# Loading the first row blocks of the output projection during the last head, and another order of its blocks

## The chip, the core and the metric

The program runs on one core of one Trainium2 chip. The metric is the device time of one execution in microseconds (us), the median of repeated runs. TensorE (PE) multiplies; its weight loads are a row of their own (PEld). VectorE (DVE), ScalarE (ACT) and GpSimd (POOL) do elementwise work, and SyncE (SP) issues most of the transfers (DMA). Each engine takes its instructions in the order of its own queue, so an instruction that waits holds up all that stand behind it on that engine.

## The reference, cut to what matters

One layer of a hybrid backbone on 512 latent tokens and 256 context tokens of width 1024, in float32. Two groups of four heads (a gated linear recurrence, "hg", and a gated delta rule, "dn") scan the tokens in both directions. Their normalised outputs are laid side by side and go through one output projection, a residual, and a mixture of 16 experts.

```
def hybrid_mixer(pc, px, lb, hg_norm_w, conv_w, a_log, dt_bias, dn_norm_w):
    ...
    hg_c, hg_x = hgrn2_branch(cols_c[:5], cols_x[:5], lb, hg_norm_w)
    dn_c, dn_x = deltanet_branch(cols_c[5:], cols_x[5:], conv_w, a_log, dt_bias, dn_norm_w)
    return jnp.concatenate([hg_c, dn_c], axis=-1), jnp.concatenate([hg_x, dn_x], axis=-1)
...
        xs = xs + g1x * (ox @ w_out[l])
        xs = xs + g2x * hierarchical_moe(modulate(rms_norm(xs, norm2_w[l]), sh2x, sc2x), *moe_args)
...
    return rms_norm(xs, final_norm_w)
```

`ox` is 512 x 1024 and `w_out` 1024 x 1024. A row block of `w_out` is 128 of its rows; blocks 0 to 3 belong to the four hg heads and blocks 4 to 7 to the four dn heads.

## The kernel before, in words

**Precision by parts.** A float32 product is made of three passes on TensorE: each operand is split into a rounded high part (a CAST on ACT) and the rest (a subtraction on DVE), and high x high, high x low and low x high are summed in PSUM. Whatever is multiplied so first needs one ACT and one DVE instruction per piece.

**Up to the projection.** The loop over heads (from L1071) runs the two scans of each head, with projections, gates (`gates`, names `z01...` and `sz`) and the rest of the modulation (`mod_rest`, tiles `wm`, L1001 loads and L1003 products) as filling. The scans' tiles live in the pool `dn`: `E` and `EB` (decay), `seg`, `kc`, `kt`, `t3`. `head_norm` (squares `nsq` on ACT L1038, a power on POOL L1045, the scaling on DVE L1047) writes the outputs in place into `ohg` and `odn`; for heads 2 and 3 this is done in the last round. After the heads the pools of the scan are closed (L1098), and `late`, `rt` and `fin` take their place.

**The output projection.** `KO` (L1109) is the order in which the eight row blocks are used, in four pairs: 0 1, 4 5, 2 3, 6 7. `channel_major` (L1111) transposes one head's output for a block on TensorE (`mt`, L1115), casts it to `mhi` (L1116) and subtracts to `mlo` (L1117). Its PSUM tile comes from the two buffers of `psG`, so a third transpose waits for the first one's `mlo`. `load_wo(nh, k2)` (L1124) loads one pair of row blocks of one half of the columns, 512 KB, into `wor` (two buffers, L1127), scales it by the gate `g1b` on DVE if it is the second half (L1130), and splits it into `woh` (L1132) and `wol` (L1134). The first half is multiplied pair by pair for four token tiles at once (L1286, PSUM `wo`, 96 products); the transposes of the last four blocks are placed behind its second pair. The second half goes token tile by token tile (L1345, 96 products), with the first half's transposes (`ptt`, L1250) and router logits (`plg`, L1258) put in between by hand. Then come the residual (L1230, L1235, L1236), the token rows `tt` written to DRAM (L1274 to L1276), the routing and the expert loop (L1404 and L1409 split weights, L1533 and L1571 multiply).

**What sets the order.** The Tile framework's scheduler orders each engine's queue from its own estimate of durations; `hi(...)` raises priority, `issue_after` and `add_manual_dep` set an order by hand. A tile put where a closed tile lay waits for the last use of that one. SP's queue carries the loads of `w_out`, the gate row `g1b` (L1141), the latent tokens `xs1` (L1143), small router rows (L1146 to L1153, `row2` among them, which TensorE transposes as `pr`, L1155), `w2b` (L1177) and the expert weights (L1204).

Of the kernel before, what the change touches and what calls it, by code (L numbers as in the profile page):

```python
# [9 lines left out]
F32 = mybir.dt.float32  # L10
F32R = mybir.dt.float32r
# [5 lines left out]
P = 128  # L17
# [203 lines left out]
def tile_kernel(ctx, tc, x, c, ctxt, c_ctx, w_mod, b_mod, norm1_w, norm2_w, w_in, w_out, hg_lb, hg_norm_w,  # L221
# [849 lines left out]
    for h in range(H):  # L1071
        with hi(HPS):
            dn_scan(h, *proj[h][:2], *prep[h][:3], prep[h][4])
        if h + 1 < H:
            with hi(HPD):
                prep[h + 1] = dn_prep(h + 1, *proj[h + 1], *dec[h + 1])
                dn_inv(h + 1, prep[h + 1][3])
        if h + 2 < H:
            dec[h + 2] = dn_decay(h + 2)
        with hi(HPG):  # L1080
            hg_head(h, vps[h // 2], *hpr[h])
        for f in FILL[h]:
            if f == "v":
                vps[1] = hg_values(1)
            elif f == "p":
                proj[h + 2] = dn_proj(h + 2)
            elif f == "q":
                hpr[h + 1] = hg_proj(h + 1)
            elif f in "01":
                sz[int(f)] = gates(int(f), h // 2)  # L1090
            elif f in "ab":
                mod_rest(1 + "ab".index(f))
            elif f in "no":
                for g in {"n": (h,), "o": (h - 1, h)}[f]:
# [11 lines left out]
    fin = mid.enter_context(tc.tile_pool(name="fin", bufs=1))  # L1106
    mhi = fin.tile([P, KB, SEQ], F32R, name="mhi")
    mlo = fin.tile([P, KB, SEQ], F32R, name="mlo")
    KO = (0, 1, 4, 5, 2, 3, 6, 7)  # L1109

    def channel_major(kb):  # L1111
        pt = psG(f"mt{kb}")
        src = (ohg, odn)[kb // 4]
        for t in range(NLT):
            nc.tensor.transpose(pt[:, t * P:(t + 1) * P], src[:, t, kb % 4, :], ident)  # L1115
        nc.scalar.copy(mhi[:, kb, :], pt)  # L1116
        nc.vector.tensor_sub(mlo[:, kb, :], pt, mhi[:, kb, :].bitcast(F32))  # L1117

    for kb in KO[:4]:
        channel_major(kb)  # L1120
    wos = [{}, {}]
    xs1 = late.tile([P, NLT, D], F32, name="xs1")

    def load_wo(nh, k2):  # L1124
# [7 lines left out]
        nc.scalar.copy(hi_, raw)  # L1132
        lo_ = fin.tile([P, 2, 512], F32R, tag="wol", name=f"wol{nh}_{k2}", bufs=NWO)
        nc.vector.tensor_sub(lo_, raw, hi_.bitcast(F32))  # L1134
        wos[nh][k2] = (hi_, lo_)
        return ld

    for k2 in KO[::2]:
        load_wo(0, k2 // 2)
    g1b = rt.tile([P, D], F32, name="g1b")  # L1140
    nc.sync.dma_start(g1b, mod_d[0].partition_broadcast(P))  # L1141
# [138 lines left out]
    for i, k2 in enumerate(KO[::2]):  # L1280
        hi_, lo_ = wos[0][k2 // 2]
        for t in range(NLT):
            ts_ = slice(t * P, (t + 1) * P)
            for k in range(2):
                for n, (m, w) in enumerate(((mhi, hi_), (mhi, lo_), (mlo, hi_))):
                    mm = nc.tensor.matmul(acc[t], m[:, k2 + k, ts_], w[:, k, :], start=(i == 0 and k == 0 and n == 0),  # L1286
                                          stop=(i == 3 and k == 1 and n == 2))
        if i == 1:
            with tc.issue_after(mm.ins):
                for kb in KO[4:]:  # L1290
                    channel_major(kb)
# [44 lines left out]
    for t in range(NLT):  # L1336
# [339 lines left out]
```

## Time and profile before

| what | value |
|---|---|
| median of 3 runs | 961.73 us (960.93 to 962.4) |
| the profiled execution | 960.25 us |
| its span, first to last instruction | 958.5 us |
| mean granted TensorE clock in it | 0.973 |
| PE busy, share of the span | 883.3 us, 92% |
| PEld | 722.3 us, 75% |
| DVE | 726.5 us, 76% |
| ACT | 501.6 us, 52% |
| POOL | 207.4 us, 22% |

Times are counted in the profiled execution from the span's start. The last head ends near 547 us, the two halves of the output projection run to 617 us, routing to about 632 us, and the experts to about 920 us. A granted clock of 1.0 is TensorE's 2.4 GHz and one of 0.5 is 1.2 GHz; a mean between them over a stretch is a mixture of the two.

### The profile page before, as it was taken

The page shows a single profiled execution, that of the slowest core. Times are in us where ns is not written, and L with a number is a line of the kernel's source. Part 1 is how long each engine was busy: PE and PEld are TensorE (multiplying, and loading weights), DVE is VectorE, ACT ScalarE, POOL GpSimd, SP SyncE. Part 2 cuts the span into 40 slices and gives each one's busy share as a digit, 9 for nine tenths or more (in the row PEclk, how much of TensorE's full clock was granted, in tenths as well). Part 3 has the DMA queues.
Part 4 walks back from the last instruction along what each step waited for, and adds up shares of the span by engine and source line. Part 5 has one row for each costly group of instructions (what it writes and reads, how often), then busy time and mean ns, then how long its engine had stood idle before and what let it go on. Part 6 is the DMA issues. An engine that isn't in the chain of part 4 may idle for free. (4 is left out here: it accounts for less than half of the span.)

```text
span 958.5 us, 20502 instructions
## 1 busy us (share of the span) xinstructions
PE 883.3 (92%) x8221; PEld 722.3 (75%) x8221; DVE 726.5 (76%) x1377; ACT 501.6 (52%) x966; POOL 207.4 (22%) x224
## 2 busy tenths in 40 slices
PE   3999998989879999799998989999999999999995
PEld 1688877878768887687895868867888887777772
DVE  2698489757899579964484566677989988888987
ACT  4445542454246344432432343127888888788862
POOL 2232631251135213412111110001111111010011
PEclk9999997999989999999999989999999999999997
DMA  9920350201102102038218278469999999999735
GB/s 313 315 67 23 111 198 24 69 22 41 30 23 52 38 25 56 12 116 251 79 51 278 70 249 327 158 248 377 382 364 365 372 368 361 374 370 363 294 129 146
DMA packets 116444, 180.03 MB, mean 188 GB/s; under 512 B 9975, under 2 KB 49459, under 8 KB 116216
## 3 DMA queue, kind: packets, MB, share of 16 engines
q1 hardware_dynamic: 109256, 163.49, 50.3%
q0 software_dynamic: 6480, 14.71, 4.6%
q8 instruction: 66, 1.08, 0.5%
q10 hardware_dynamic: 608, 0.47, 0.2%
q14 instruction: 34, 0.28, 0.1%
HBM read 170.31 MB, written 16.27 MB: 195 GB/s over the span
## 5 line engine op out<-in xcount | busy, mean ns | idle before, releaser
L1409 DVE TENSOR_TENSOR lo<-w,hi 128x1024 fp32r<-128x1024 f32 x184 | 216.8, 1222 | 27.1 <-ACT hi L1404 25.3
L1404 ACT CAST hi<-w 128x1024 fp32r<-128x1024 f32 x184 | 186.1, 1050 | 22.0 <-PE pu L1533 9.7
L1571 PE MATMUL py<-lo,ah 128*128 128x512 f32 x128 | 51.8, 404 | 0.7
L1571 PE MATMUL py<-hi,ah 128*128 128x512 f32 x128 | 50.8, 398 | 0.0
L1571 PE MATMUL py<-hi,al 128*128 128x512 f32 x128 | 49.4, 396 | 0.3 <-DVE al L1563 0.3
L1533 PE MATMUL pg<-lo,xh 128*128 128x512 f32 x120 | 48.7, 406 | 0.0
L1533 PE MATMUL pu<-lo,xh 128*128 128x512 f32 x120 | 48.3, 403 | 0.2 <-DVE lo L1409 0.2
L1533 PE MATMUL pg<-hi,xh 128*128 128x512 f32 x120 | 47.7, 397 | 0.0
L1533 PE MATMUL pu<-hi,xh 128*128 128x512 f32 x120 | 47.6, 396 | 0.0
L1533 PE MATMUL pg<-hi,xl 128*128 128x512 f32 x120 | 47.5, 396 | 0.0
L1533 PE MATMUL pu<-hi,xl 128*128 128x512 f32 x120 | 47.5, 396 | 0.0
L1389 POOL DMA_INDIRECT y_d<-y,cl x15 | 17.5, 1168 | 133.2 <-ACT y L1575 119.9
L815 POOL TENSOR_TENSOR am<-atr,cst 128x128 f32<-128x128 f32 x32 | 17.7, 557 | 123.4 <-PE po L818 108.5
L1382 POOL DMA_INDIRECT xg<-t_d,cl x15 | 18.4, 1230 | 115.9 <-PE xt L1521 106.1
L938 DVE TENSOR_TENSOR KS<-KS,F 128x384 f32<-128x384 f32 x56 | 32.3, 615 | 3.3 <-ACT km L901 2.8
L811 DVE TENSOR_SCALAR vs<-px,bs 128x128 f32<-128x128 f32 x48 | 16.6, 345 | 19.5 <-PE px L809 19.3
L1571 PEld LDWEIGHTS py<-lo,ah 128*128 128x128 f32 x128 | 24.1, 188 | 8.6 <-DVE lo L1409 3.3
L1003 PE MATMUL psm<-wm,cl 128*32 128x128 f32 x512 | 25.4, 284 | 4.8 <-DMA wm<-in_w_mod_dram 4.4
L562 DVE SCALAR_TENSOR_TENSOR qc<-lpad,cw,qc 128x512 f32<-128x512 f32 x32 | 29.4, 919 | 0.4
L1571 PEld LDWEIGHTS py<-hi,ah 128*128 128x128 f32 x128 | 24.1, 188 | 6.3 <-ACT ah L1562 0.6
L1571 PEld LDWEIGHTS py<-hi,al 128*128 128x128 f32 x128 | 24.2, 189 | 6.2 <-DVE al L1563 0.8
L1533 PEld LDWEIGHTS pu<-lo,xh 128*128 128x128 f32 x120 | 22.6, 188 | 7.9 <-DVE lo L1409 2.8
(1065 smaller groups left out, 2723.8 us busy)
## 6 DMA issues: line engine op xcount, KB each, us to landing
w<-in_w_gate_dram SPq DMA_DIRECT2D x32, 1024.0 KB, 15.1
w<-in_w_up_dram SPq DMA_DIRECT2D x32, 1024.0 KB, 14.9
w<-in_w_down_dram SPq DMA_DIRECT2D x32, 1024.0 KB, 16.5
wm<-in_w_mod_dram SPq DMA_DIRECT2D x64, 256.0 KB, 4.3
wm<-in_w_mod_dram SPq DMA_DIRECT2D x16, 512.0 KB, 8.3
y_d<-zt POOLq DMA_DIRECT2D x8, 512.0 KB, 7.7
wor<-in_w_out_dram SPq DMA_DIRECT2D x8, 512.0 KB, 5.1
xt<-in_x_dram SPq DMA_DIRECT2D x4, 512.0 KB, 9.9
```

The source lines that it names most:

```text
L562: nc.vector.scalar_tensor_tensor(al, s, w, al, op0=ALU.mult, op1=ALU.add)
L811: nc.vector.tensor_scalar(vs, px[:, 0:P], bs[:, d, i:i + 1], None, op0=ALU.mult)
L815: nc.gpsimd.tensor_mul(am, atr[:, t, :], K(("le", "ge")[d]))
L938: nc.vector.tensor_mul(kh, kh, tt(d, 1 - d))
L1003: nc.tensor.matmul(ps[32 * c_:32 * c_ + 32, P * j:P * j + P], cl[:, kb, :], raw[:, P * c_:P * c_ + P], start=(kb == 0), stop=(kb == KB - 1))
L1382: return nc.gpsimd.indirect_dma_start(out=dst, out_offset=None, in_=t_d[:, :], in_offset=bass.IndirectOffsetOnAxis(ap=idx, axis=0), bounds ...
L1389: i_ = nc.gpsimd.indirect_dma_start(out=y_d[:, :], out_offset=bass.IndirectOffsetOnAxis(ap=idx, axis=0), in_=src, in_offset=None, bounds_c ...
L1404: nc.scalar.copy(hi, raw)
L1409: s.append(lo_on.tensor_sub(s[1], raw, s[0].bitcast(F32)))
L1533: a_pu[0] = nc.tensor.matmul(ps, m[:, kb, :], ww[:, k, :], start=(kb == 0 and n == 0), stop=(kb == KB - 1 and n == 2))
L1571: mm = nc.tensor.matmul(ps, m[:, k, :], ww[:, k % 2, :], start=(k == 0 and n == 0), stop=(k == 3 and n == 2))
```

## The change

Two row blocks of the first column half, blocks 0 and 1, are no longer loaded by `load_wo`. Each is loaded alone (256 KB) into the scan's own buffers (`E` and `seg`) and split there (`EB` and `t3` for the high parts, `kc` and `kt` for the rest), in code that stands in front of the closing of the scan's pools. `load_wo` makes the other three pairs, in the order 4 5, 6 7, 2 3. The order of the blocks in both halves is 0 1 4 5 6 7 2 3. Six blocks (0, 1, 4, 5, 6 and 2) are transposed in front of the first half, and one each (7, then 3) behind its first and second pair. The split of the pair 4 5 is ordered by hand behind that of block 1. The weights are now indexed as lists of two blocks.

```
+    first_wo = [[], []]
+    for k in range(2):
+        raw = dn.tile([P, 512], F32, tag=("E", "seg")[k], name=f"wor_{k}")
+        nc.sync.dma_start(raw, w_out[k * P:(k + 1) * P, 0:512])
+        hi_ = dn.tile([P, 512], F32R, tag=("EB", "t3")[k], name=f"woh_{k}")
+        lo_ = dn.tile([P, 512], F32R, tag=("kc", "kt")[k], name=f"wol_{k}", bufs=2)
+        nc.scalar.copy(hi_, raw)
+        nc.vector.tensor_sub(lo_, raw, hi_.bitcast(F32))
+        first_wo[0].append(hi_)
+        first_wo[1].append(lo_)
     mix.close()
...
-    KO = (0, 1, 4, 5, 2, 3, 6, 7)
+    KO = (0, 1, 4, 5, 6, 7, 2, 3)
...
-    for kb in KO[:4]:
-        channel_major(kb)
-    wos = [{}, {}]
+    parts_of = [channel_major(kb) for kb in KO[:5] + KO[6:7]]
+    wos = [{0: first_wo}, {}]
...
+        if nh == 0 and k2 == KO[2] // 2:
+            for a_, b_ in zip((h_, l_), parts_of[1]):
+                tc.add_manual_dep(a_.ins, b_.ins.name, behind, reason="behind what is ready")
...
-    for k2 in KO[::2]:
+    for k2 in KO[2::2]:
         load_wo(0, k2 // 2)
...
-        if i == 1:
+        if i < 2:
             with tc.issue_after(mm.ins):
-                for kb in KO[4:]:
-                    channel_major(kb)
+                channel_major(KO[5 + 2 * i])
```

Lines behind the insertion have higher numbers in the changed kernel: L1116 is L1127 there, L1117 is L1128, L1130 is L1141, L1132 is L1143, L1134 is L1145, L1143 is L1157 and L1152 is L1166. Numbers at the end of a name tell tiles apart; `wor_0`, `wor_1`, `wor_2` and `wor_3` are the pairs 0 1, 2 3, 4 5 and 6 7.

On ACT, at the end of the last head, the queue before had the first pair's cast ahead of the first transposed block:

```order
L969 COPY kst_4_1_7139<-hpk_4_1_7137 128x128
L1132 CAST woh_0_7389<-wor_0_7387 128x1024
L1116 CAST mhi<-mt_7358 128x512
L1132 CAST woh_2_7395<-wor_2_7393 128x1024
L1116 CAST mhi<-mt_7365 128x512
L1038 ACTIVATE nsq_7314,nss_7315<-odn 128x128 x4
```

and with the change:

```order
L969 COPY kst_4_1_7139<-hpk_4_1_7137 128x128
L1127 CAST mhi<-mt_7370 128x512
L1127 CAST mhi<-mt_7377 128x512
L1143 CAST woh_2_7415<-wor_2_7413 128x1024
L1143 CAST woh_3_7421<-wor_3_7419 128x1024
L1038 ACTIVATE nsq_7314,nss_7315<-odn 128x128
L1127 CAST mhi<-mt_7384 128x512
```

Both transposed blocks now stand ahead of every weight cast there.

On DVE, in the middle of the first half, where the second half's first pair (`wor_0` with `g1b`) is scaled, before:

```order
L1047 SCALAR_TENSOR_TENSOR ohg<-ohg,nss_7329,sz_7151 128x128 x4
L1130 TENSOR_TENSOR wor_0_7447<-wor_0_7447,g1b 128x1024
L1157 COPY col_7428<-pr_7426 128x24
L1130 TENSOR_TENSOR wor_2_7454<-wor_2_7454,g1b 128x1024
L1159 COPY A_162<-col_7428 128x8
L1160 SCALAR_TENSOR_TENSOR A_162<-col_7428 128x8
L1117 TENSOR_TENSOR mlo<-mt_7557,mhi 128x512
L1134 TENSOR_TENSOR wol_0_7452<-wor_0_7447,woh_0_7450 128x1024
```

and with the change:

```order
L1047 SCALAR_TENSOR_TENSOR ohg<-ohg,nss_7329,sz_7151 128x128 x4
L1145 TENSOR_TENSOR wol_1_7429<-wor_1_7425,woh_1_7427 128x1024
L1141 TENSOR_TENSOR wor_0_7467<-wor_0_7467,g1b 128x1024
L1128 TENSOR_TENSOR mlo<-mt_7398,mhi 128x512
L1145 TENSOR_TENSOR wol_0_7472<-wor_0_7467,woh_0_7470 128x1024
L1128 TENSOR_TENSOR mlo<-mt_7405,mhi 128x512
L1128 TENSOR_TENSOR mlo<-mt_7553,mhi 128x512
L1128 TENSOR_TENSOR mlo<-mt_7584,mhi 128x512
L1141 TENSOR_TENSOR wor_2_7474<-wor_2_7474,g1b 128x1024
L1171 COPY col_7448<-pr_7446 128x24
```

One scaling instead of two stands ahead of the low parts of the late blocks, and the router's column (`col`) comes behind all of them.

On SP, the loads behind the gate row `g1b`, before:

```order
L1150 DMA rb<-in_b_expert_dram 128x16
L1152 DMA row_7423<-mod_d 16x128
L1153 DMA row_7423<-in_norm_w_dram 8x128
L1127 DMA wor_0_7447<-in_w_out_dram 128x2x512
L1127 DMA wor_2_7454<-in_w_out_dram 128x2x512
L1175 DMA sh_7475<-mod_d 128x1024
L1143 DMA xs_7386<-in_x_dram 128x1024 x4
```

and with the change:

```order
L1138 DMA wor_0_7467<-in_w_out_dram 128x2x512
L1155 DMA g1b<-mod_d 128x1024
L1160 DMA wrt<-in_w_group_dram 128x8x4
L1161 DMA wrt<-in_w_expert_dram 128x8x16
L1163 DMA rb<-in_b_group_dram 128x4
L1164 DMA rb<-in_b_expert_dram 128x16
L1157 DMA xs_7412<-in_x_dram 128x1024 x4
L1166 DMA row_7443<-mod_d 16x128
L1167 DMA row_7443<-in_norm_w_dram 8x128
L1138 DMA wor_2_7474<-in_w_out_dram 128x2x512
L1189 DMA sh_7495<-mod_d 128x1024
```

The second half's first pair moved ahead of `g1b`, and the four loads of the latent tokens moved ahead of the small `row` loads.

Further moves: on SP the two new loads stand in the first `mod_rest`, one behind its 6th load `wm` and one behind its 20th; `w2b` moves behind all five expert weights and behind `g2b` and `fw`. On TensorE `pr` stands behind 68 of the first half's 96 products, and the router's constant (`pcb`, L1167) moves from the first half into the second half's first tile. On DVE the token rows of the first two tiles, and the row `a2` (L1178) that they need, move behind the second half's second tile.

## Rows read from the trace of the kernel before

**Rows 1.** Stretches of the span (from : to and length in us), busy us and number of instructions of PE, PEld, DVE, ACT and POOL, then the granted clock, the DMA share and GB/s: the end of the last head and the first half of the output projection.

```profile
545.00:550.00 5.00, 3.04 (x24) 2.45 (x22) 2.63 (x10) 1.37 (x2) 0.68 (x1) 1.00 0.68 210
...
550.00:555.00 5.00, 4.79 (x16) 3.75 (x17) 4.15 (x8) 4.69 (x17) 1.04 (x1) 0.67 0.44 122
...
568.00:572.00 4.00, 1.16 (x7) 1.06 (x8) 4.00 (x7) 2.84 (x4) 2.00 (x1) 1.00 1.01 394
...
572.00:576.00 4.00, 4.00 (x14) 3.17 (x13) 2.40 (x4) 0.09 (x1) 0.00 (x0) 0.57 1.02 405
```

**Rows 2.** PE in order of time (start, us, what, how many; in brackets the idle time before it and what ended it): from the transposes of block 1 to the first products of the first half.

```profile
547.48 0.60 PE L1115 MATMUL mt<-cst,ohg 128*128 128x128 f32 x4
...
550.21 0.96 PE L1286 MATMUL wo<-woh,mhi 128*128 128x512 f32 x3 [2.13 <-ACT mhi L1116]
...
553.94 0.63 PE L1286 MATMUL wo<-woh,mhi 128*128 128x512 f32 x1
...
554.37 0.63 PE L1286 MATMUL wo<-wol,mhi 128*128 128x512 f32 x1
...
555.20 0.39 PE L1286 MATMUL wo<-woh,mhi 128*128 128x512 f32 x1
...
555.42 0.39 PE L1286 MATMUL wo<-wol,mhi 128*128 128x512 f32 x1
```

**Rows 3.** ACT in order of time in the same place, and the last two squares of the last head.

```profile
548.63 1.04 ACT L1132 CAST woh<-wor 128x1024 fp32r<-128x1024 f32 x1 [3.79 <-DMA wor<-in_w_out_dram]
...
549.58 0.58 ACT L1116 CAST mhi<-mt 128x512 fp32r<-128x512 f32 x1
...
555.65 0.31 ACT L1038 ACTIVATE nsq<-ohg 128x128 f32<-128x128 f32 x1
...
556.08 0.31 ACT L1038 ACTIVATE nsq<-ohg 128x128 f32<-128x128 f32 x1
...
556.30 0.18 ACT L1038 ACTIVATION_READ_ACCUMULATOR nsq<-ohg 128x1 f32 x1
```

**Rows 4.** SP's transfers in order of issue (start, time of the issues, line, number), and the last line of the answer on the tile `row`: from issue to landing.

```profile
544.00 7.32 SPq L1127 DMA_DIRECT2D wor<-in_w_out_dram  x3
...
556.51 0.34 SPq L1141 DMA_DIRECT2D g1b<-mod_d  x1
...
561.09 0.43 SPq L1152 DMA_DIRECT2D row<-mod_d  x1
...
563.50 2.40 SPq L1143 DMA_DIRECT2D xs<-in_x_dram  x4
...
571.85 2.35 SPq L1127 DMA_DIRECT2D wor<-in_w_out_dram  x2
...
577.57 0.90 SPq L1177 DMA_DIRECT2D w2b<-in_norm_w_dram  x1
...
DMA to landing us min/median/max: 2.4/2.4/2.4
```

**Rows 5.** PE in order of time: the second stop in the first half, what follows it, the second half's first product, and its first transposes.

```profile
566.83 0.39 PE L1286 MATMUL wo<-wol,mhi 128*128 128x512 f32 x1
...
570.84 0.63 PE L1115 MATMUL mt<-cst,odn 128*128 128x128 f32 x4 [3.62 <-DVE mlo L1117]
...
572.24 0.62 PE L1286 MATMUL wo<-woh,mhi 128*128 128x512 f32 x1
...
575.64 1.86 PE L1167 MATMUL pcb<-wrt,shb 128*128 128x20 f32 x16
...
584.20 0.39 PE L1345 MATMUL wo<-woh,mhi 128*128 128x512 f32 x1
...
587.41 0.66 PE L1250 MATMUL ptt<-cst,xs 128*128 128x128 f32 x4 [1.24 <-DVE xs L1236]
```

**Rows 6.** DVE in order of time: the scaling of the last hg head, the scaling of the second half's first pair, and the low part behind it.

```profile
560.31 1.13 DVE L1047 SCALAR_TENSOR_TENSOR ohg<-ohg,nss,sz 128x128 f32<-128x128 f32 x4
...
566.61 1.23 DVE L1130 TENSOR_TENSOR wor<-wor,g1b 128x1024 f32<-128x1024 f32 x1 [5.17 <-DMA wor<-in_w_out_dram]
...
570.02 0.68 DVE L1117 TENSOR_TENSOR mlo<-mt,mhi 128x512 fp32r<-128x512 f32 x1
```

**Rows 7.** DVE in order of time in the second half: the row `a2` (a pass over 128x1024), the residual of the first tile, and the last instructions ahead of the last residual.

```profile
593.19 1.22 DVE L1178 SCALAR_TENSOR_TENSOR a<-a,w2b 128x1024 f32<-128x1024 f32 x1
...
594.43 0.69 DVE L1230 TENSOR_TENSOR xs<-xs,wo 128x512 f32<-128x512 f32 x1
...
616.81 0.23 DVE L1263 SCALAR_TENSOR_TENSOR lg<-lg,B,cb 128x20 f32<-128x20 f32 x1
...
617.42 0.69 DVE L1230 TENSOR_TENSOR xs<-xs,wo 128x512 f32<-128x512 f32 x1 [0.38 <-PE wo L1345]
```

**Rows 8.** Waits of SP's queue from 560 to 940 us (who waited for whom: us in total, times, longest): the expert weights.

```profile
SPq L1204 <- DVE lo L1409: 163.7, 60, 10.9
...
SPq L1204 <- PE wo L1345: 0.2, 1, 0.2
```

**Rows 9.** The first `mod_rest`: SP's loads in order of time, the last use of `E` (all four heads; durations in ns, then first and last start), and PE behind the last of these loads.

```profile
419.84 23.89 SPq L1001 DMA_DIRECT2D wm<-in_w_mod_dram  x26
...
L674 DVE TENSOR_TENSOR atr<-pqk,E x4: 680/681/686, 136.4 to 425.9; 128x512 f32<-128x512 f32 x4
...
444.12 0.41 PE L1003 MATMUL psm<-wm,cl 128*32 128x128 f32 x4 [0.40 <-DMA wm<-in_w_mod_dram]
```

More of the change, by code (lines that the diff above doesn't have):

```diff
@@ L1115, in channel_major @@
             nc.tensor.transpose(pt[:, t * P:(t + 1) * P], src[:, t, kb % 4, :], ident)
-        nc.scalar.copy(mhi[:, kb, :], pt)
-        nc.vector.tensor_sub(mlo[:, kb, :], pt, mhi[:, kb, :].bitcast(F32))
-    for kb in KO[:4]:
-        channel_major(kb)
-    wos = [{}, {}]
+        h_ = nc.scalar.copy(mhi[:, kb, :], pt)
+        return h_, nc.vector.tensor_sub(mlo[:, kb, :], pt, mhi[:, kb, :].bitcast(F32))
+    behind = mybir.DependencyInfo(mybir.DependencyClass.NoSync, mybir.DependencyReason.DATA)
+    parts_of = [channel_major(kb) for kb in KO[:5] + KO[6:7]]
+    wos = [{0: first_wo}, {}]
     xs1 = late.tile([P, NLT, D], F32, name="xs1")
@@ L1131, in load_wo @@
         hi_ = fin.tile([P, 2, 512], F32R, tag="woh", name=f"woh{nh}_{k2}", bufs=NWO)
-        nc.scalar.copy(hi_, raw)
+        h_ = nc.scalar.copy(hi_, raw)
         lo_ = fin.tile([P, 2, 512], F32R, tag="wol", name=f"wol{nh}_{k2}", bufs=NWO)
-        nc.vector.tensor_sub(lo_, raw, hi_.bitcast(F32))
-        wos[nh][k2] = (hi_, lo_)
+        l_ = nc.vector.tensor_sub(lo_, raw, hi_.bitcast(F32))
+        if nh == 0 and k2 == KO[2] // 2:
+            for a_, b_ in zip((h_, l_), parts_of[1]):
+                tc.add_manual_dep(a_.ins, b_.ins.name, behind, reason="behind what is ready")
+        wos[nh][k2] = [[w[:, k, :] for k in range(2)] for w in (hi_, lo_)]
         return ld
-    for k2 in KO[::2]:
+    for k2 in KO[2::2]:
         load_wo(0, k2 // 2)
@@ L1285, in tile_kernel @@
                 for n, (m, w) in enumerate(((mhi, hi_), (mhi, lo_), (mlo, hi_))):
-                    mm = nc.tensor.matmul(acc[t], m[:, k2 + k, ts_], w[:, k, :], start=(i == 0 and k == 0 and n == 0),
+                    mm = nc.tensor.matmul(acc[t], m[:, k2 + k, ts_], w[k], start=(i == 0 and k == 0 and n == 0),
                                           stop=(i == 3 and k == 1 and n == 2))
-        if i == 1:
+        if i < 2:
             with tc.issue_after(mm.ins):
-                for kb in KO[4:]:
-                    channel_major(kb)
+                channel_major(KO[5 + 2 * i])
     for t in range(NLT):
@@ L1310, in pick @@
         return mm
-    behind = mybir.DependencyInfo(mybir.DependencyClass.NoSync, mybir.DependencyReason.DATA)
     chained = [mm]
@@ L1344, in tile_kernel @@
                     part(*todo.pop(0)[1:])
-                put(nc.tensor.matmul(acc1, m[:, kb, ts_], w[:, kb % 2, :], start=(i == 0 and n == 0),
+                put(nc.tensor.matmul(acc1, m[:, kb, ts_], w[kb % 2], start=(i == 0 and n == 0),
                                      stop=(i == KB - 1 and n == 2)))
```

## The prediction

> **What bounds the kernel now.** I read the table of stretches first, for where TensorE is idle or slowed, then the order of time on PE, ACT, DVE and SP around those places, and last SP's waits in the expert loop. Between the last head and the second half of the output projection TensorE stops twice, and each stop is paid twice. The first: block 1 is transposed by 548.08, the first product starts at 550.21, 2.13 us idle [rows 2]. It waits for `mhi`, but the cause stands one step back: on ACT the cast of the first weights is queued ahead of `mhi` and waits 3.79 us for a load issued at 544.00 [rows 3, 4]; `mhi` itself could have run from about 547.5. Behind the stop the granted clock is a mixture (0.67) and products start 0.43 us apart, at 1.2 GHz, until 555.2; then 0.22 to 0.23 us apart [rows 1, 2]. In those 5.0 us twelve products and four transposes ran, 12 x 0.225 + 4 x 0.1 = 3.1 us at full clock, so the slow clock costs 1.9 us. The second stop: PE runs dry at 567.22 and resumes at 570.84, 3.62 us [rows 5]. It waits for a PSUM buffer, which waits for `mlo`, which stands on DVE behind the scaling of the second half's weights, and that waited 5.17 us for its load [rows 6]. Afterwards again 0.57 of the clock [rows 1], about eight products 0.2 us late each, 1.6 us. A third stop of 1.24 us stands ahead of the second half's first `ptt` [rows 5]. Together 2.13 + 1.9 + 3.62 + 1.6 + 1.24 = 10.5 us in a stretch that TensorE otherwise fills.
>
> **What is won at the start.** With blocks 0 and 1 split long before, ACT casts `mhi` of block 0 as soon as its transposes end, about 547.45, takes 0.58 us [rows 3], and the first product follows the second transposes without a gap, at about 548.1. The 2.13 us go, and with them, I take it, the 1.9 us, because PE is then busy from 545 on where before it was busy for 3.04 of 5 us [rows 1]. Before block 4 is wanted, PE has eight products from the new tiles and then twelve more; the pair 4 5 is loaded as the first pair was (issued 544.00, there at 548.63) and split by about 552, while PE asks for it at 554.3. This load is hidden.
>
> **What becomes of the second stop.** I carry the queues on with the durations of the rows: product 0.227 us, four transposes 0.4, cast 1.05 or 0.58, DVE pass 1.22 (128x1024) or 0.69. The late blocks' `mlo` now stand behind one scaling, not two, and that scaling needs `g1b`. `g1b` waits for the last square on ACT, which ended at 556.48 [rows 3] and was followed by its issue at 556.51 [rows 4]. With the new ACT order that square ends at 548.63 + 2.1 (two weight casts) + 0.6 (`mhi`) + 8 x 0.43 (squares, by the starts of two [rows 3]) = 554.8. A load of this size lands 4.6 us after issue (544.00 to 548.63), so `g1b` is there at 559.5; DVE arrives at 559.1, scales until 560.7, and `mlo` of block 6 is ready at 561.4. PE wants the PSUM buffer behind it at 562.3. The next buffer needs the cast and subtraction of `wor_0` as well: 563.7 against 563.6. So the stop closes, with next to no slack.
>
> **What is late next: `pr`.** On SP the four `xs` loads (2.4 us of issues) now stand ahead of `row` [rows 4]. From `g1b` to `row` it took 4.6 us of issues; now `xs` starts at 554.9 + 4.6 = 559.5 and `row` at 561.9. Behind bulk on one queue it can land no earlier than 2.1 MB at 0.39 MB per us (394 to 405 GB/s [rows 1]) allow: 559.5 + 2.4 + 5.4 = 567.3. PE reaches `pr` behind 68 products and six sets of transposes: 548.1 + 15.4 + 2.4 = 565.9. I charge the 1.4 us. If `row` overtook the bulk it would land at 561.9 + 2.4 = 564.3 and the stop would be nil; at 300 GB/s it would be 3 us. The Trainium skill, "DMA: Bandwidth & Descriptors", section "Queues, rings and completion order", says that descriptors of one queue are taken in ring order on each DMA engine; by that rule the load waits behind the `xs` bulk and the change pays for the move, without it the forecast would be 1.4 us lower. No row of the kernel before has a small load behind bulk, so none decides it.
>
> The first half then ends at 567.3 + 28 x 0.227 = 573.7, against 584.2 before [rows 5].
>
> **The second half's weights.** These do not come earlier in the same measure. The second pair's load is issued behind `row` and lands near 568.6; scaling 1.22, router column and `wra` 1.5, subtraction 1.22 bring DVE to 572.6. Only then is its buffer free, so the last load goes out at 572.6, practically when it did before (571.85 [rows 4]), and lands at 577.2. DVE scales it (578.4), does a residual (0.69) and then the low part of pair 6 7: 580.3. PE asks for that at 573.7 + 8 products (1.8) + `pcb` 1.9 [rows 5] + 0.4 + 5 products (1.1) = 578.9, so it waits 1.4 us. The last pair is ready when wanted. At this point the account is 10.5 - 1.4 - 1.4, and about 0.5 for near misses: 7.2 us. Carrying PE's queue through to the first tile's end I get 585.5, where before DVE's add behind it began at 594.43 [rows 7], so about 594.2: 8.7 us; the account leaves out some slow products and small gaps. I use 7.5.
>
> **DVE's tail.** `a2` needs `w2b`, which is now issued behind five weight loads, `g2b` and `fw`: 7.3 MB from about 574.3, at 0.39 MB per us there at 593.1; DVE wants it at 585.5 + 9.3 (one tile) + 0.7 = 595.5. This cover is 2.4 us thick. But the token rows of tiles 0 and 1 (four passes of about 1.22 us) now stand in one piece behind the second tile, ahead of the third tile's residual, and the routing chain behind that. Before, DVE was done at 617.04 and waited 0.38 us for PE's last tile [rows 7]; now it reaches that residual about 1.1 us behind PE. 7.5 - 1.1 = 6.4.
>
> **In the scans.** Two loads, two casts of about 0.58 and two subtractions of 0.69 us are added there, the same bytes and passes as are saved later. ACT and DVE have room. One load lands while DMA is idle; the other enters a stream of 26 loads that take 23.89 us, 0.92 each, whose last one PE waits for (0.40 us) [rows 9]. I charge 0 to 0.92, and take 0.4. The scheduler also rearranged PE between the third and the last head with the same instructions; bounds for that, from the small gaps there, are about -1 to +1.5, taken as 0.
>
> **Does it reach the end?** Routing follows the last residual. In the expert loop SP waits 163.7 us for DVE to free weight buffers [rows 8], so its loads follow the compute; PE's release of the projection's tiles cost it 0.2. I see no fixed clock behind it, so the shift of 6.0 us is kept. Against the profiled execution: 960.25 - 6.0 = 954.25; its own time lies 1.48 under the median, so the median becomes 961.73 - 6.0 = **955.7**.
>
> **Rivals.** (a) *The new waits keep TensorE slow.* Two stops of 1.4 us come where a stop of 2.13 and one of 3.62 were followed by half clock and one of 1.24 was not [rows 2, 5]. If both are followed by it, 1.9 + 1.6 go back, and half a microsecond for a late `g1b`: 2.0 won, 959.7. For it: no slack at the PSUM buffers. Against: both are shorter than those that were punished. (b) *SP's queue is held by the early load.* The load of block 0 waits in SP's queue for the last use of `E`, at 426.6, and stands where SP arrives at about 432.7: 6.1 us of slack. The loads behind it (12 `wm`, then the third head's weights) all wait with it, and PE has little else there. Each us beyond the slack costs about one. It decides from 6.1 + 6.0 = 12.1 us of lateness; then the kernel is slower. At 15 it gives 961.73 + 2.9 = 964.6. Against: PE's new order has the last head's inverse earlier, not later. (c) *The expert stream is not shifted.* If the loads' start and not PE sets the end, all is covered and the time stays at 961.7. Against: [rows 8].
>
> **How the numbers follow.** Forecast 0.70 (won 3.5 to 9.5: from 6.0, up by the missing `pr` stop 1.4, the DVE tail 1.1 and 1 of order; down by 2.5 for one slow stretch), rival (a) 0.16, (b) and other disorder in the scans 0.07, (c) 0.07. The range reaches from 6.0 + 3.5 = 9.5 won, 952.2, to rival (a) with a little, 959.9. A measurement here tells 0.2%, 1.9 us, from no change. Faster by more than that: the forecast and half of (a), which lies on that bound, 0.79; within it: (c) and the rest of (a), 0.14; slower: 0.07.
>
> **What would show it.** In the changed profile: the first product within 0.3 us of the second transposes, at full clock; no wait of DVE for `wor` above 1 us ahead of the late `mlo`; a stop of 0 to 3 us at `pr`; the first half's end at 572 to 576; a wait of PE for `wol` some five products behind `pcb`; `a2` without a wait; the last residual 5 to 8 us earlier; the expert loop as long as before. It is wrong if PE is late already at 547, if the second stop returns under another name, or if the last residual is early and the end is not.

## The result, and the profile of the changed kernel

The changed kernel takes 952.5 us (median), the kernel before beside it 961.8; the ratio is 0.9917, with a 95% interval of 0.9901 to 0.9934, so between 6.3 and 9.5 us are won. The profiled execution of the changed kernel took 952.88 us, with a span of 951.1; that of before 960.25 and 958.5. A second timing, told below, gave 0.9912 (0.9885 to 0.9939). The forecast was 955.7, a gain of 6.0: the sign was right, 952.5 lies just inside the range (952.2 to 959.9), and the size was 2 to 3 us short (8.0 by the ratio, 9.2 between the medians).

TensorE in stretches, as in [rows 1]; the last column but two is the granted clock:

```profile
545.00:550.00 5.00, 4.91 (x31) 4.03 (x31) 4.23 (x12) 3.26 (x6) 0.00 (x0) 1.00 0.54 196
550.00:555.00 5.00, 5.00 (x25) 4.11 (x24) 3.48 (x10) 4.78 (x19) 2.08 (x2) 1.00 0.64 198
565.00:570.00 5.00, 3.02 (x14) 2.21 (x13) 1.43 (x2) 0.00 (x0) 0.00 (x0) 1.00 1.03 343
570.00:575.00 5.00, 5.00 (x23) 4.14 (x23) 4.74 (x9) 1.37 (x2) 1.06 (x1) 1.00 0.71 244
```

Both stretches that had a mixed clock before (0.67 in the second row's stretch, 0.72 in the fourth's) are now at full clock, 2.4 GHz, and only 565 to 570 has idle time to speak of. The queue of PE in order of time, the answer to [rows 2, 5]:

```profile
546.69 0.60 PE L1126 MATMUL mt<-cst,ohg 128*128 128x128 f32 x4
547.35 0.51 PE L1300 MATMUL wo<-woh,mhi 128*128 128x512 f32 x1
...
565.60 0.39 PE L1300 MATMUL wo<-wol,mhi 128*128 128x512 f32 x1
567.96 0.21 PE L1169 MATMUL pr<-cst,row 24*128 24x24 f32 x1 [1.98 <-DMA row<-in_norm_w_dram]
...
574.58 0.39 PE L1357 MATMUL wo<-woh,mhi 128*128 128x512 f32 x1
...
576.40 1.85 PE L1181 MATMUL pcb<-wrt,shb 128*128 128x20 f32 x16
...
579.91 0.50 PE L1357 MATMUL wo<-wol,mhi 128*128 128x512 f32 x1
```

The first product starts 0.06 us after the second set of transposes ends (546.69 + 0.60). One stop is left in the first half, 1.98 us ahead of `pr`, and the row before it carries no wait. The second half begins at 574.58 instead of 584.20, but `pcb` (1.85 us), which stood in the first half before (575.64 [rows 5]), now comes behind that point: of the 9.6 us between the two starts 7.8 are won. At 579.91 the weights of pair 6 7 are asked for, and there is no wait to speak of. On ACT, against [rows 3]:

```profile
546.71 1.20 ACT L1127 CAST mhi<-mt 128x512 fp32r<-128x512 f32 x2 [2.66 <-DMA wor<-in_w_out_dram]
547.81 2.00 ACT L1143 CAST woh<-wor 128x1024 fp32r<-128x1024 f32 x2
```

The two `mhi` now run ahead of the weight casts. (The wait of 2.66 is put down to the DMA that was last by the profile; PE's transposes released it.) On SP, against [rows 4]:

```profile
559.50 1.80 SPq L1157 DMA_DIRECT2D xs<-in_x_dram  x4
561.34 0.55 SPq L1166 DMA_DIRECT2D row<-mod_d  x1
561.94 0.35 SPq L1167 DMA_DIRECT2D row<-in_norm_w_dram  x1
```

and on DVE, against [rows 6, 7]:

```profile
559.23 1.23 DVE L1141 TENSOR_TENSOR wor<-wor,g1b 128x1024 f32<-128x1024 f32 x1 [1.69 <-DMA g1b<-mod_d]
...
564.79 0.69 DVE L1128 TENSOR_TENSOR mlo<-mt,mhi 128x512 fp32r<-128x512 f32 x1 [0.68 <-ACT mhi L1127]
569.05 1.23 DVE L1141 TENSOR_TENSOR wor<-wor,g1b 128x1024 f32<-128x1024 f32 x1 [3.57 <-DMA wor<-in_w_out_dram]
...
585.43 0.68 DVE L1244 TENSOR_TENSOR xs<-xs,wo 128x512 f32<-128x512 f32 x1
...
595.41 1.22 DVE L1192 SCALAR_TENSOR_TENSOR a<-a,w2b 128x1024 f32<-128x1024 f32 x1
596.67 2.36 DVE L1288 TENSOR_TENSOR tt<-xs,a 128x1024 f32<-128x1024 f32 x2
598.94 2.48 DVE L1289 SCALAR_TENSOR_TENSOR tt<-tt,B,sh 128x1024 f32<-128x1024 f32 x2
...
611.53 0.69 DVE L1244 TENSOR_TENSOR xs<-xs,wo 128x512 f32<-128x512 f32 x1 [1.74 <-PE wo L1357]
```

DVE still waits 3.57 us for the second pair's weights, but now behind the last `mlo` and not ahead of it, and nobody misses it there. The first tile ends 9.0 us earlier (585.43 against 594.43), the last 5.9 (611.53 against 617.42). So 3.1 us are given back in between. PE shows where:

```profile
606.75 0.41 PE L121 MATMUL ppos<-sel,cst 128*128 128x32 f32 x2 [1.03 <-DVE sel L115]
```
```profile
608.00:611.00 3.00, 3.00 (x9) 2.35 (x9) 1.77 (x4) 0.00 (x0) 0.00 (x0) 0.51 0.42 164
```

DVE takes the token rows of tiles 0 and 1 in one piece (596.67 to 601.4), then the third residual and the routing chain (`sel` is at its end); PE waits 1.03 us for `sel` at the chain's end, and behind it eight products go at half clock (some 0.43 us each instead of 0.23, 1.6 us). At the last residual it is DVE that waits for PE (1.74 us).

To see the size of a step beside what differs from one execution to the next, here are the stages of all profiles, in us, worked out from the times at which these rows of the timeline start: the row with the last `po` products of the scans, the first product of the projection, the second half's first product, the first and the last second-half residual on DVE, the first and the last expert product, the span's end. "Again" and "pair" are further profiles of the same kernel; the experiments follow. Two columns need care: `pcb` (1.85 us) lies in the first half in before, before_again, order_only, order_pin, row_first, both and xs_late2, and behind it, in the first tile, in the other six. Between the two groups only the sum of "first half" and "to first residual" can be compared.

| profile | scans | to first product | first half | to first residual | to last residual | routing | experts | tail | span |
|---|---|---|---|---|---|---|---|---|---|
| before | 547.2 | 3.0 | 34.0 | 10.2 | 23.0 | 16.1 | 301.7 | 23.4 | 958.5 |
| before_again | 548.5 | 2.8 | 33.9 | 10.2 | 23.0 | 16.2 | 301.7 | 23.5 | 959.8 |
| after | 546.5 | 0.9 | 27.2 | 10.8 | 26.1 | 15.1 | 301.7 | 22.8 | 951.1 |
| after_again | 546.0 | 0.9 | 26.5 | 10.9 | 25.6 | 16.4 | 301.7 | 22.8 | 950.8 |
| after_pair | 547.4 | 0.9 | 27.2 | 10.8 | 25.1 | 15.1 | 301.6 | 23.0 | 951.1 |
| early_only | 547.6 | 0.9 | 27.0 | 17.5 | 24.3 | 15.1 | 301.7 | 22.4 | 956.5 |
| order_only | 548.4 | 2.9 | 32.5 | 8.9 | 24.3 | 15.9 | 307.5 | 22.7 | 963.0 |
| order_pin | 546.2 | 3.1 | 32.1 | 8.9 | 24.3 | 16.8 | 300.7 | 23.6 | 955.7 |
| row_first | 548.0 | 0.9 | 27.0 | 10.5 | 23.2 | 16.8 | 300.6 | 23.7 | 950.6 |
| w2b_first | 545.1 | 0.9 | 27.4 | 10.9 | 22.7 | 15.6 | 300.6 | 23.5 | 946.8 |
| w2b_pair | 545.6 | 0.9 | 26.7 | 11.1 | 22.4 | 18.3 | 302.4 | 23.6 | 951.0 |
| both | 547.9 | 0.9 | 27.0 | 11.8 | 23.0 | 15.6 | 300.6 | 23.7 | 950.4 |
| xs_late2 | 546.5 | 0.9 | 27.0 | 12.8 | 23.0 | 16.7 | 300.7 | 23.5 | 951.1 |

From the means of the first two and the next three rows: scans 1.2 won, start 2.0, first half 7.0, first tile 0.6 lost, the other tiles 2.6 lost, routing 0.6 and tail 0.6 won, experts nothing: 8.2 us. With `pcb` in the same place the first half wins 5.1 and the first tile 1.2.

### The profile page after: what moved, and what is told of

The parts are those of the page before. It is cut to its first block, busy times and chain, and to the rows that moved or that the text cites. A ratio compares the mean times of both kernels' runs of the same rounds, so it can differ in the third digit from the quotient of the medians.

```text
span 951.1 us, 20500 instructions
## 1 busy us (share of the span) xinstructions
PE 876.7 (92%) x8221; PEld 717.0 (75%) x8221; DVE 725.6 (76%) x1378; ACT 501.8 (53%) x967; POOL 208.6 (22%) x224
## 5 line engine op out<-in xcount | busy, mean ns | idle before, releaser
L1421 DVE TENSOR_TENSOR lo<-w,hi 128x1024 fp32r<-128x1024 f32 x184 | 216.7, 1220 | 27.3 <-ACT hi L1416 25.6
L1401 POOL DMA_INDIRECT y_d<-y,cl x15 | 17.5, 1168 | 133.2 <-ACT y L1587 119.9
L815 POOL TENSOR_TENSOR am<-atr,cst 128x128 f32<-128x128 f32 x32 | 17.8, 558 | 116.7 <-PE po L818 100.4
## 6 DMA issues: line engine op xcount, KB each, us to landing
w<-in_w_up_dram SPq DMA_DIRECT2D x32, 1024.0 KB, 15.6
```

Source lines behind the costliest of these rows:

```text
L815: nc.gpsimd.tensor_mul(am, atr[:, t, :], K(("le", "ge")[d]))
L1401: i_ = nc.gpsimd.indirect_dma_start(out=y_d[:, :], out_offset=bass.IndirectOffsetOnAxis(ap=idx, axis=0), in_=src, in_offset=None, bounds_c ...
L1421: s.append(lo_on.tensor_sub(s[1], raw, s[0].bitcast(F32)))
```

## The experiments

Times are medians, each beside the kernel before on the same chip; ratios have their 95% interval.

| kernel | us | before, us | ratio |
|---|---|---|---|
| early_only | 956.6 | 960.4 | 0.9945 (0.992 to 0.9971) |
| order_only | 964.43 | 960.4 | 1.004 (1.0017 to 1.0063) |
| order_pin | 958.38 | 962.13 | 0.997 (0.9951 to 0.999) |
| row_first | 952.09 | 962.13 | 0.9897 (0.9865 to 0.993) |
| w2b_first | 950.94 | 962.13 | 0.9887 (0.985 to 0.9924) |
| both | 952.34 | 962.13 | 0.9914 (0.9884 to 0.9945) |
| after_pair | 952.5 | 960.83 | 0.9912 (0.9885 to 0.9939) |
| w2b_pair | 952.48 | 960.83 | 0.9905 (0.9877 to 0.9933) |
| xs_late2 | 953.03 | 960.83 | 0.992 (0.9893 to 0.9947) |

### Each half of the change alone

**early_only**, against the changed kernel:

```
-    KO = (0, 1, 4, 5, 6, 7, 2, 3)
+    KO = (0, 1, 4, 5, 2, 3, 6, 7)
-    parts_of = [channel_major(kb) for kb in KO[:5] + KO[6:7]]
+    parts_of = [channel_major(kb) for kb in KO[:4]]
...
-        if i < 2:
+        if i == 1:
             with tc.issue_after(mm.ins):
-                channel_major(KO[5 + 2 * i])
+                for kb in KO[4:]:
+                    channel_major(kb)
```

> The first two blocks are loaded and split early, block order and late transposes stay as before. Theory 'two separate stops': the first product follows the second transposes at full clock (2.13 us idle and 1.9 us of slow clock gone, first product near 547.4); a stop of 1.5 to 3 us comes back behind the last late blocks, because the fourth mlo stands on VectorE behind the second scaling, whose load lands near 568.5. Time 3.5 to 6 us under the kernel before, 955.7 to 958.2. Rival 'early load is everything': 952 to 953.5, as the whole change. Rival 'the gain is in the scans': the last head's end is as early as in the changed kernel and the rest is as long as before, so 960.5 to 961.

956.6 us, 3.8 under before: inside what "two separate stops" gave. The first half is as short as in the whole change (27.0; it has no stop ahead of `pr`), so the early load by itself takes away the start's stop and the slow clock behind it, and leaves 1.61 us of the second stop's 3.62, with full clock behind it. But the first tile of the second half takes 17.5 us instead of 10.8. DVE's and PE's queues, and PE's clock:

```profile
570.43 1.22 DVE L1141 TENSOR_TENSOR wor<-wor,g1b 128x1024 f32<-128x1024 f32 x1 [3.40 <-DMA wor<-in_w_out_dram]
571.58 0.68 DVE L1128 TENSOR_TENSOR mlo<-mt,mhi 128x512 fp32r<-128x512 f32 x1
...
578.61 1.23 DVE L1141 TENSOR_TENSOR wor<-wor,g1b 128x1024 f32<-128x1024 f32 x1 [2.17 <-DMA wor<-in_w_out_dram]
...
581.49 0.69 DVE L1250 TENSOR_TENSOR xs<-xs,tm 128x512 f32<-128x512 f32 x1
```
```profile
563.14 0.50 PE L1300 MATMUL wo<-woh,mhi 128*128 128x512 f32 x1 [1.61 <-ACT mhi L1127]
...
582.23 1.11 PE L1264 MATMUL ptt<-cst,xs 128*128 128x128 f32 x4 [3.06 <-DVE xs L1250]
```
```profile
580.00:585.00 5.00, 2.77 (x9) 2.39 (x10) 4.96 (x9) 2.57 (x5) 0.00 (x0) 0.52 1.05 399
585.00:590.00 5.00, 5.00 (x20) 4.42 (x19) 2.28 (x7) 1.67 (x5) 0.00 (x0) 0.50 1.04 387
```

The wait of DVE for the second pair's weights again stands ahead of a late `mlo`, everything behind it on DVE is later, the first half's first residual (581.49) too, and PE waits 3.06 us for that, with half clock until 590 behind it. So the old third stop [rows 5] is back and larger. What the new order is worth with the early load in place is the difference to the whole change: 3 us by the ratios, 4 to 5 by the medians.

**order_only**: the new `KO` and the moved transposes; blocks 0 and 1 are loaded by `load_wo` as before.

```
-    first_wo = [[], []]
-    for k in range(2):
...
-    wos = [{0: first_wo}, {}]
+    wos = [{}, {}]
-    for k2 in KO[2::2]:
+    for k2 in KO[::2]:
```

> New block order and moved transposes, all four pairs of the first half loaded late as before. Theory 'two separate stops': the first product waits about 2 us and runs at half clock for some 3 us as before; the stop of 3.62 us behind the late blocks closes or falls under 1 us. Time 3 to 5.5 us under the kernel before, 956.2 to 958.7. Rival 'the order only helps with the early load': a stop of 2 to 3.6 us is found at the late blocks, 960 to 962. Rival 'early load is nothing': 952 to 953.5.

964.4 us, slower than before by 1.7 to 6.3 per thousand, which no theory had. By the table the projection is 1.5 us shorter in the first half, 1.3 to the first residual and 1.3 longer in the other tiles; what makes it slower is the expert part, 307.5 instead of 301.7. The wait of SP's queue at the branch at the experts' start, and what PE waits for behind it, before and then in order_only:

```profile
SPq L1448 <- SPq L1448: 4.7, 1, 4.7
```
```profile
650.81 0.66 PE L1554 MATMUL at<-cst,a 128*128 128x128 f32 x4 [1.69 <-DVE a L1545]
```
```profile
SPq L1450 <- SPq L1450: 10.4, 3, 6.0
```
```profile
649.49 1.09 PE L1523 MATMUL xt<-cst,xg 128*128 128x128 f32 x8 [2.79 <-DMA xg<-t_d,cl]
655.48 1.12 PE L1556 MATMUL at<-cst,a 128*128 128x128 f32 x4 [4.90 <-DVE a L1547]
```
```profile
652.81 1.28 ACT L1546 ACT_TABLE_LOAD   x1 [14.64 <-DMA xg<-t_d,cl]
```

Before, one expert weight load stands ahead of the branch in SP's queue. Here the scheduler had put two more there, issued at 639.86 and 641.40. By the trace's semaphore events SP passes the branch when what it issued ahead of it has landed: before, the one load lands at 644.94 and SP's wait for it ends at 644.96; here the three land at 646.00, 649.07 and 652.42, and the last two waits end at 649.09 and 652.43. ACT goes on at 652.81, DVE's `a` follows ACT and PE's `at` follows `a`: PE stands for 2.79 and 4.90 us instead of 1.69, 6.0 us more, as much as the expert part is longer (5.8). **order_pin** holds these two loads behind the branch, where before has them:

```
-    for i in range(4):
-        load_weights()
+    i4 = len(raws)
+    for i in (i4, i4 + 2):
+        load_weights(i)
...
     tc.add_manual_dep(branch, picked.ins.name, behind, reason="behind the second expert's tokens")
+    for i in (i4 + 1, i4 + 3):
+        load_weights(i)
```

> The new block order and moved transposes alone, as in order_only, but two expert weight loads that the scheduler had put ahead of the branch at the experts' start are held behind it, as in the kernel before. Theory 'the 5.9 us that order_only lost lie at the branch': from the first expert's first product to the last expert product it takes 301.7 us again instead of 307.5, the first half of the projection is 1 to 2 us shorter than before, and the time is 1 to 2.5 us under the kernel before, some 958 to 960.5. Rival 'the order alone costs': the expert part stays over 304 us, 961 to 964.

958.4 us against 962.1, and 300.7 us for the experts: the loss lay at the branch. (With the edit the scheduler also swaps some instructions inside the expert loop: in the kernels that have it, all but w2b_pair, the experts take 300.6 or 300.7 us and the tail 23.5 to 23.7, 324.1 to 324.3 together, where the changed kernel has 324.5 or 324.6.) The order alone wins 1 to 4.7 us by its interval, but not by what the forecast said. Its queues, PE, DVE and ACT:

```profile
549.31 1.65 PE L1291 MATMUL wo<-woh,mhi 128*128 128x512 f32 x3 [2.33 <-ACT mhi L1117]
...
570.48 0.50 PE L1291 MATMUL wo<-woh,mhi 128*128 128x512 f32 x1 [2.09 <-ACT mhi L1117]
```
```profile
565.85 1.23 DVE L1131 TENSOR_TENSOR wor<-wor,g1b 128x1024 f32<-128x1024 f32 x1 [4.84 <-DMA wor<-in_w_out_dram]
```
```profile
547.73 1.04 ACT L1133 CAST woh<-wor 128x1024 fp32r<-128x1024 f32 x1 [3.98 <-DMA wor<-in_w_out_dram]
```

The start is as before (2.33 us, behind a cast that waits 3.98 for its load). The second stop is 2.09 us, with 0.31 ahead of it and 0.46 behind it on PE, where before has 3.62, so the moved transposes alone close less than half of it: without the early load the whole chain of loads is one pair later, DVE's 4.84 us for a second-half load stand ahead of a late `mlo` again, and the late `mhi` stand on ACT behind the casts of both scaled pairs. But the slow clock behind the second stop is gone (1.00 in 570 to 575, 0.72 before). The closing of the second stop belongs to both halves of the change together. The stop ahead of `ppos` is in each half alone too (1.03 in early_only, 1.04 in order_pin), and the tiles take 24.3 us in each of them where before takes 23.0: DVE has the token rows in one piece there as well.

**before_again** and **after_again**:

> The kernel before once more, unchanged. If the 0.9 us by which the changed kernel is ahead at 517 us (a wait of 1.87 us for wm at 506.15 and slow clock behind it) and the 0.7 us in the last 20 us (slow clock from 940 on) belong to the run and not to the change, one or both are missing here; if they belong to the kernel, both come back within 0.2 us.

961.57 us. In [rows 9] and the next 80 us the two profiles of before differ by themselves: in the second the modulation's first batch of products (418 to 454 us) takes 3.3 us longer, while a wait of 1.87 us for `wm` near 506 and the slow clock behind it are missing. The tail's slow clock is back (23.5). So a single profile tells nothing of the scans below about 1.3 us.

> The changed kernel once more, unchanged. If slow clock in the tail and behind waits for wm is a matter of the run, it may appear here; the stop at pr (1.98 us), the stop ahead of ppos (1.03 us) and the slow clock behind it from 608 to 611.3 should come back if the kernel makes them.

952.75 us; the stop ahead of `pr` is 1.19, that ahead of `ppos` 1.04 with half clock behind it, both the kernel's own.

### The two waits that the changed kernel keeps

**row_first** issues the row loads ahead of `xs` (and, like the kernels below it but after_pair, holds the two expert loads as order_pin does).

```
-    for t in range(NLT):
-        nc.sync.dma_start(xs1[:, t, :], x[t * P:(t + 1) * P, :])
...
-    nc.sync.dma_start(row2[16:24, :], norm2_w[0].rearrange("(k p) -> k p", p=P))
+    row_ld = nc.sync.dma_start(row2[16:24, :], norm2_w[0].rearrange("(k p) -> k p", p=P))
+    with tc.issue_after(row_ld.ins):
+        for t in range(NLT):
+            nc.sync.dma_start(xs1[:, t, :], x[t * P:(t + 1) * P, :])
```

> The changed kernel, but the two small row loads are issued ahead of the four xs loads (and the two expert loads held behind the branch as in order_pin, where the changed kernel has them anyway). Theory 'row waits behind the xs bulk': the stop ahead of pr (1.98 us in one profile, 1.2 in the other) goes to under 0.2, the second half starts 1.2 to 2 us earlier, and 0.5 to 2 us of it reach the end: 950.5 to 952 where the changed kernel has 952.5. Rival 'the stop moves': VectorE's wait for the second half's weights, whose load stands behind the same bulk, stops TensorE by as much some products later, 952 to 953.

952.1 us. The stop ahead of `pr` is gone, and another is in its place (PE):

```profile
563.75 0.24 PE L1170 MATMUL pr<-cst,row 24*128 24x24 f32 x1
...
580.66 0.50 PE L1359 MATMUL wo<-wol,mhi 128*128 128x512 f32 x1 [1.18 <-DVE wol L1145]
```

The rival held: the second half's weights come behind the same `xs` bulk, and a TensorE that is earlier waits for them: from the first product to the first residual row_first takes 37.5 us, the changed kernel 37.4 to 38.1. So the row does wait behind the bulk (1.98, 1.19, 1.90, 1.75 and 1.41 us in the five profiles with the new block order and `xs` ahead of `row`, none in the three with `row` first), and taking that stop away is worth nothing that can be measured at the end. The eight profiles agree with the rule of the Trainium skill that the prediction weighed ("DMA: Bandwidth & Descriptors", section "Queues, rings and completion order": on each DMA engine a queue's descriptors are taken in ring order). Row_first is not a test of the row load alone: in it the scheduler also issued `w2b` earlier (577.57, 582.63 in the changed kernel) and put the token rows of the first two tiles back between the residuals, so the stop ahead of the first `ppos` is gone here too and the tiles take 23.2 us.

**w2b_first** lets `w2b` go out ahead of the expert weights:

```
-    nc.sync.dma_start(w2b, norm2_w[0].partition_broadcast(P))
+    w2_ld = nc.sync.dma_start(w2b, norm2_w[0].partition_broadcast(P))
...
-    with tc.issue_after(last_wo.ins):
+    with tc.issue_after(last_wo.ins), tc.issue_after(w2_ld.ins):
```

> The changed kernel, but the load of w2b is issued ahead of the five expert weight loads, so that a2 and the token rows of tile 0 run on VectorE before tile 1 is done (the two expert loads at the branch as in order_pin). Theory 'the DVE tail costs the end': the stop of 1.03 us ahead of ppos and the half clock behind it (1.6 us) go, the last residual comes 2 to 2.7 us earlier than in the changed kernel, the time is 950 to 951. Rival 'the slow clock only moves': it then falls on the routing products as in the kernel before, and the time is 951.5 to 953.

**both** has this and row_first's edit.

> The row loads first and w2b first, together. If both theories hold the gains add: 948.5 to 950.5. If either stop only moves, 951 to 953.

w2b_first: 950.9 us, the tiles take 22.7 us instead of 25.1 to 26.1 and there is no stop ahead of the first `ppos`. both: 952.3; the tail of the tiles is as short (23.0), but two stops (0.83 for a residual, 1.25 for weights) stand in the first tile. The gains do not add; by the schedule just told, row_first had the shorter tiles already.

**after_pair** and **w2b_pair** were timed side by side to see whether w2b_first is ahead at all:

> The changed kernel again, timed beside the two below on one chip: 952 to 953.5, 7.5 to 9.5 us under the kernel before. It shows whether w2b_first is really ahead of it.

> w2b_first again. Theory 'the DVE tail costs the end': the projection's four tiles take 22.7 to 23.1 us from the first second-half residual to the last, as in w2b_first, where the changed kernel takes 25.6 to 26.1, and the time is 1 to 3 us under after_pair. Rival 'run to run': the two are within 0.5 us.

952.5 and 952.5. The tiles are 2.7 us shorter again (22.4 against 25.1), and the time is the same: the stage behind them took 18.3 us instead of 15.1. The first stretches of the routing, windows of w2b_first and of w2b_pair, then PE in w2b_first and in w2b_pair:

```profile
610.00:614.00 4.00, 4.00 (x23) 4.00 (x23) 3.13 (x20) 0.00 (x0) 0.00 (x0) 0.57 0.99 361
616.00:622.00 6.00, 5.72 (x52) 5.53 (x51) 5.33 (x37) 1.41 (x6) 0.00 (x0) 1.00 1.05 388
```
```profile
610.00:614.00 4.00, 2.70 (x24) 2.51 (x23) 3.34 (x22) 0.00 (x0) 0.00 (x0) 1.00 1.00 376
616.00:622.00 6.00, 6.00 (x31) 6.00 (x32) 4.66 (x36) 0.49 (x4) 0.00 (x0) 0.54 1.05 387
```
```profile
610.09 4.55 PE L1318 MATMUL xT<-Oe,xs 128*128 128x128 f32 x24
...
615.08 0.38 PE L121 MATMUL ppos<-sel,cst 128*128 128x32 f32 x2 [0.44 <-DVE ov L130]
```
```profile
609.77 2.92 PE L1318 MATMUL xT<-Oe,xs 128*128 128x128 f32 x24
614.76 0.60 PE L121 MATMUL ppos<-sel,cst 128*128 128x32 f32 x2 [2.06 <-DVE ov L130]
...
616.03 6.88 PE L1318 MATMUL xT<-Oe,xs 128*128 128x128 f32 x36
```

One kernel, two executions. In w2b_first the half clock fell on products that DVE's routing chain covers anyway (24 in 4.55 us; `ppos` comes 8.1 us behind the last residual in either execution). In w2b_pair those ran at full clock, PE then waited 2.06 us for DVE, and the half clock came behind the wait, on products that the experts wait for (36 of them in 6.88 us). The rival, that the slow clock moves, holds for this run; whether w2b_first is worth a microsecond on the average stays open.

**xs_late2** is w2b_first with `row`, then the second pair of the second half's weights, then `xs` on SP's queue, and that pair's scaling behind the last `mlo`:

```
         last_wo = load_wo(1, k2 // 2)
+        if k2 == KO[2]:
+            with tc.issue_after(last_wo.ins):
+                for t in range(NLT):
+                    nc.sync.dma_start(xs1[:, t, :], x[t * P:(t + 1) * P, :])
...
+    for ins in scaled:
+        tc.add_manual_dep(ins, parts_of[-1][1].ins.name, behind, reason="behind the last low part")
```

> w2b_first, and on SyncE's queue row first, then the second pair of the second half's weights, then xs; the scaling of that pair stands behind the last low part. Theory 'both stops come from the place behind the xs bulk': the stop ahead of pr (1.75 us in w2b_first) goes and the stop for wol of row_first (1.2 us) does not come in its place; the first tile of the second half ends 1.2 to 1.8 us earlier after the first product than in w2b_first, and the time is 1 to 2 us under it. Rival 'the next wait takes it': xs lands later and the residuals or the last pair's weights stop TensorE for as long, no change against w2b_first.

953.0 us, no gain. The stop ahead of `pr` is gone, and PE waits 0.85 us for a residual and 1.14 at the third pair's weights; the first tile takes 12.8 us (with half clock again, 0.67 in 580 to 585), and from the first product to the first residual it is 39.7 us against 38.3 in w2b_first. The rival held here too. No version that I ran is shown to beat the changed kernel.

## Why the prediction was right, and where its size was off

**Start: right.** To the first product 0.9 us instead of 2.9 and full clock behind it. early_only and order_pin show that this part belongs to the early load alone.

**Second stop: right in time, incomplete in cause.** `g1b` was to land at 559.5 and did at 559.2, the `mlo` of block 6 to be ready at 561.4 and was at 561.1; the stop is gone. The prediction put this down to the new place of the transposes; the two halves alone show that it needs both (1.61 us left in early_only, 2.09 and two small stops in order_pin). The first half as a whole, with `pcb` set right, is 5.1 us shorter; with the 2.0 of the start that is 7.1, and 3.62 + 1.9 + 1.6 + 2.13 less the stop at `pr` (1.7 in the mean of three) is 7.6.

**`pr`: right.** 1.4 forecast, 1.98, 1.19 and 1.90 measured.

**Weights of pair 6 7: wrong.** A wait of 1.4 us was charged, none over 0.2 is there: PE asks at 579.7 and not at 578.9 (the 68 products and six sets of transposes ahead of `pr` took 18.6 us instead of 17.8, and the stop 1.98 instead of 1.4, while the scans ended 0.8 earlier), and DVE is done at 579.9, not at 580.3. Errors of 0.8 and 0.4 us in a difference of two queues made up the wait.

**First tile: mis-sized by 0.9.** 7.5 us were used where the carried queue gave 8.7. From the last `po` product to the first residual it is 47.1 us before and 38.7 after: 8.4. The carried queue was the better figure.

**DVE's tail: the cause right, the path and the size not.** The token rows in one piece do make DVE late; -1.1 was charged and it is -2.6 (25.6 against 23.0, means of three and two profiles). The forecast had DVE reach the last residual behind PE; there DVE waits 1.74 us for PE. I followed the residual alone. The routing chain stands behind it, PE waits for the chain's end (1.03 us), and the stop brings half clock onto eight products (1.6 us). w2b_first takes this away and gets the 2.9 us at the last residual.

**Scans: the largest error.** 0.4 us of loss was charged, with -1 to +1.5 for the scheduler's rearrangement taken as 0. The scans end 1.2 us earlier. With the early load (nine profiles) they end at 546.7 in the mean, without it (four) at 547.6, each with a standard deviation of about 1: 0.8 won, not a loss, though 0 is not excluded. Steadier is the stage in which it happens: the modulation's first batch of products takes 30.2 to 31.4 us in all nine (30.8 in the mean) and 31.6 to 34.9 in all four (33.2), so the two groups all but touch; of the 2.5 us between the means 1.6 are lost again around it. The block order of the projection is not the cause: early_only is with the nine, order_only and order_pin are with the four. In the traces PE works through the scans in the changed kernel's order in all nine and in that of before in all four, so load and rearrangement always came together, and which of them does it stays open.

**To the end: right, with a small thing unseen.** The expert part is 301.7 us in both, so the shift is kept. Routing and tail are 0.6 us shorter each, the routing with a spread of 1.3 between profiles of the changed kernel (15.1 to 16.4). Before, TensorE had half clock in routing (0.51 from 620 to 627); now less of it falls there (0.66 from 614 to 619), while another part comes ahead of the last residual and is counted as the tiles' loss.

The sum with measured terms is 8.4 - 2.6 + 1.2 + 0.6 + 0.6 = 8.2 us, against 7.5 - 1.1 - 0.4 = 6.0. Terms were too low by 0.9, 1.6 and 1.2 us and too high by 1.5, so they partly cancel: that the total came within 2.2 us is in part luck. (In the chances, half of 0.16 with 0.70 is 0.78, not 0.79.)

**The rivals.** (a) fell: the stop ahead of `pr` is as long as the punished one of before (2.13), and the clock stays at 1.00 behind it. Half clock behind a new wait did come at another place, behind the 1.03 us ahead of `ppos`, for 1.6 us. (b) fell: the load of block 0 goes out at 432.08 as said, without a wait; that of block 1 waits longer (4.6 us), in front of a load that waits 23.9 us for PE anyway. SP's queue in that stretch, against [rows 9]:

```profile
396.57 0.33 SPq L1102 DMA_DIRECT2D wor<-in_w_out_dram  x1
420.66 11.32 SPq L1001 DMA_DIRECT2D wm<-in_w_mod_dram  x14
432.08 0.38 SPq L1102 DMA_DIRECT2D wor<-in_w_out_dram  x1
```

(c) fell: SP's waits in the expert loop, against [rows 8], are the same kind, and PE's part in them is small:

```profile
SPq L1218 <- DVE lo L1421: 157.2, 59, 10.9
...
SPq L1218 <- PE wo L1357: 1.5, 1, 1.5
```

## What to carry to other kernels

A load that an in-order engine's first split waits for is best taken out of the queue altogether: hoisted into buffers that are dead for the time, it closed the stop, the slow clock behind it and more than half of the next stop (1.61 us left of 3.62); the order of what follows then decides whether the gain is kept (early_only 3.8 us, the whole change 8 to 9). When a queue gets earlier, look next for work that another engine had been doing in the shadow of the old stop: here DVE's token rows and routing chain, which took 2.6 us back. And compare the whole order of the queues after any local edit: two loads that a scheduler moved ahead of a branch, where SP then waited for them to land, cost 5.8 us, 70 us behind the code that was changed.

## What the runs showed of the hardware that I had not expected

The granted clock does not follow from the length of the last stop. Stops of 2.13 and 3.62 us before were followed by half clock, and 1.98 us ahead of `pr` was not (1.00 in 565 to 575); 1.03 us ahead of `ppos` was, in two of three profiles of the changed kernel (1.03 and 1.04), and in the third 1.57 us at the same place was not (1.00 in 605 to 615); from 615 to 620 the clock was down in all three (0.67, 0.73, 0.66). A wait of 2.07 us in routing was followed by 0.62 in 618 to 621 in row_first, and by 1.00 up to 630 in the kernel with both edits. In one kernel, w2b_first, the same few microseconds of half clock fell on covered work in one execution (routing 15.6 us) and on the chain in the other (18.3). A gain of one or two microseconds in such a stretch can't be read from one profile.
